# Tail of a one-layer hybrid decoder step: two of the last eight multiplications on POOL, their stores from ACT's queue, the last addition and square in halves

## The chip, the cores and the metric

The kernel runs on one core of a Trainium2 chip. The metric is the device time of one execution in microseconds, as the median of several runs. Five engines work side by side, each with its own instruction stream: PE (matrix multiplication), DVE (vector), ACT (scalar and activation functions), POOL (general SIMD) and SP (here it only issues DMAs). They meet only through semaphores. Matrix products are written to PSUM; everything else lives in SBUF, and outputs go to HBM by DMA.

## The reference, cut to what matters

One layer of a decoder: a normalised input goes through a projection, a gated convolution and a retention mixer, an output projection, and then a feed-forward block. The outputs are the final normalisation of the residual stream and the new states. The change lies wholly in the last two lines of this:

```python
x = x + concat([conv_out, ret_out]) @ w_out
xn = _rmsnorm(x, norm2_g)
x = x + (silu(xn @ w_gate) * (xn @ w_up)) @ w_down
...
# _rmsnorm(x, g): x * rsqrt(mean(x * x) + EPS) * g
y = _rmsnorm(x, final_norm_g)
```

## The kernel before, in words

The residual stream is held transposed: 1024 features as 8 row blocks (`m`, 0 to 7) of 128 partitions, and 1056 tokens as columns in two sets (`s`), each in two column groups (`g`). The last column group is `s` = 1, `g` = 1, with `n` = 256 columns. `x1[m][g]` holds the sum so far of a row block.

Nearly all of the time goes into matrix products in which each operand is split into a high and a low part, so that three products stand for one. The down projection is done in blocks of inner tiles; its last block, the loop over `s`, `g` and `m` at the end, takes 12 products per row block into a PSUM bank `ps` (line 1001). Then, for that row block, DVE adds the bank to `x` (line 1006), ACT squares `x` into `q` (`sq3`, line 1011; line 1008 for `m` = 0) and scales `x` by the gain of the final norm (line 1014), and DVE sums the squares into `ss3` (line 1013). The square of the last row block isn't added: it goes to the norm as a second operand.

`finish` normalises one column group. `rms_compact` (line 213) has PE multiply `ss3` and then `q`, 128 columns at a time, by a vector of ones: two products each, which bring the sum over partitions. DVE, ACT and DVE again make the reciprocal root from it, on 128x2 elements (lines 222, 224 and 198 to 202). PE spreads it over all partitions into the PSUM tile `pb`, called `n3b` in the trace (line 981). Then DVE multiplies each of the 8 row blocks by `pb` into `yt` (line 986), and after every two of them SP issues one store of 256 KB (line 987).

`finish` is a generator. Its steps for one column group are drawn between the products of the next group (`next(tail, None)`); those of the last group have no products left to hide behind. The framework that builds the program orders the instructions of each engine, finds out from the tiles what each must wait for, and puts in the semaphores. The `fin` pool keeps four `yt` buffers, and five small ones that `ss3` and `sq3` share. SP's stream ends with waits for all outstanding DMAs, and then all engines meet at a barrier (line 115).

Of the kernel before, what the change touches and what calls it, by code (L numbers as in the profile page):

```python
# [12 lines left out]
AF = mybir.ActivationFunctionType  # L13
ALU = mybir.AluOpType
AX = mybir.AxisListType

P = 128
# [14 lines left out]
KT = DM // P  # L32
# [6 lines left out]
SETS = 2  # L39
# [8 lines left out]
SO = [0, 272]  # L48
# [65 lines left out]
def _build(nc, t, offs, ncols):  # L114
    with tile.TileContext(nc) as tc:
        _body(nc, tc, t, offs, ncols)


def _body(nc, tc, t, offs, ncols):
    PSUM = bass.MemoryType.PSUM  # L120
    V, S, G, T, D = nc.vector, nc.scalar, nc.gpsimd, nc.tensor, nc.sync
    HW = SG // 2
    with contextlib.ExitStack() as ctx:
# [23 lines left out]
        gf = gains[:, 2 * KT:3 * KT]  # L147
# [15 lines left out]
        def split_w(ap, n=1024):  # L163
            return [split_u(load_w(ap[:, o:min(n, o + 512)], min(512, n - o)), min(512, n - o))
                    for o in range(0, n, 512)]
# [11 lines left out]
        def bank(name):  # L177
            return acc.tile([P, 2, 512], F32, tag="acc", name=name)
# [10 lines left out]
        def proj(w, xs, s, width, name, fill=None):  # L189
            ps = bank(name)  # L190
            for k in range(len(xs)):
                mm_k(ps, w, k, xs[k], s, width, k == 0, k == len(xs) - 1)
                if fill is not None and k % 2 == 1:
                    next(fill, None)
            return pg(ps, s, width)
# [8 lines left out]
        def rms_compact(sets, name):  # L204
            blocks = [(i, o, min(P, w - o)) for i, (_, w) in enumerate(sets) for o in range(0, w, P)]
            tot = len(blocks)
            ps = aux.tile([P, 512], F32, tag="aux", name=name + "p")
            a = cst.tile([P, 16], F32, tag="rms", name=name + "a", bufs=6)
            V.memset(a, 1.0)
            nq = len(sets[0][0])  # L210
            for q in range(nq):
                for i, (c, o, n) in enumerate(blocks):
                    T.matmul(ps[:n, q * tot + i:q * tot + i + 1], sets[c][0][q][:, o:o + n], ones[:, 0:1],
                             start=True, stop=True)
            for q in range(nq):
                i = 0
                while i < tot:
                    j, n = i, blocks[i][2]
                    while j < tot and blocks[j][2] == n:
                        j += 1  # L220
                    if q == 0:
                        V.tensor_scalar(a[:n, i:j], ps[:n, i:j], 1.0 / DM, EPS, ALU.mult, ALU.add)
                    else:
                        V.scalar_tensor_tensor(a[:n, i:j], ps[:n, q * tot + i:q * tot + j], 1.0 / DM, a[:n, i:j],
                                               ALU.mult, ALU.add)
                    i = j
            r = cst.tile([P, 16], F32, tag="rms", name=name + "r", bufs=6)
            tmp = cst.tile([P, 16], F32, tag="rms", name=name + "t", bufs=6)
            rsqrt(r[:, :tot], a[:, :tot], tmp[:, :tot])
            return r, blocks  # L230
# [17 lines left out]
        with contextlib.ExitStack() as mid_ctx:  # L248
# [74 lines left out]
            for k in range(KT):  # L323
                for s in range(SETS):
                    n = WALL[s]
# [25 lines left out]
            for s in range(SETS):  # L351
                n = WALL[s]
# [42 lines left out]
            for j in range(4):  # L395
                w = w_in(C_V + j)
                for s in range(SETS):
                    ps = proj(w, xn[s], s, WALL[s], "pv")
# [263 lines left out]
        def gg(name):  # L662
            return late.tile([P, SG], F32, tag="gg", name=name, bufs=9)
# [8 lines left out]
        for f in range(4):  # L672
            w = w_in(C_G + f)
            for s in range(SETS):
                n = WTOK[s]
                ps = proj(w, xn[s], s, n, "pg")
                x = gg("gt")
# [29 lines left out]
        for s in range(SETS):  # L707
            n = ntok[s]
            ss2 = late.tile([P, SG], F32, tag="rr", name="ss2", bufs=3)
            half = None  # L710
            for m in range(KT):
                x = gg("x1")
                D.dma_start(x[:, :2 * n], t["x"][m * P:(m + 1) * P, OFF[s]:OFF[s] + 2 * n])
                ps = proj(split_w(t["w_out"][m]), mix[s], s, 2 * n, "po")
# [28 lines left out]
                else:  # L743
                    q = gg("sq")
# [126 lines left out]
        x1 = [[None] * 2 for _ in range(KT)]  # L871
        for f in range(NFF):
# [34 lines left out]
            for g in range(2):  # L907
                x, y = gt[g][:, :HT], up[g][:, :HT]
# [19 lines left out]
        def tf(name):  # L928
            return fin.tile([P, HW], F32, tag="tt", name=name, bufs=5)
# [42 lines left out]
        yo = t["o_y"].rearrange("(m p) n -> p m n", p=P)  # L972

        def finish(s, g, ss3, q):
            n = ntok[s]
            oc = slice(OOFF[s] + g * n, OOFF[s] + (g + 1) * n)
            r, blocks = rms_compact([([ss3, q], n)], "n3")
            yield
            pb = aux.tile([P, 512], F32, tag="aux", name="n3b")
            for i, (_, o, w) in enumerate(blocks):  # L980
                T.matmul(pb[:, o:o + w], r[:w, i:i + 1].broadcast_to([w, P]), ident[:w, :w], start=True, stop=True)
            for m in range(0, KT, 2):
                yt = fin.tile([P, SG], F32, tag="yt", name="yt", bufs=4)
                y2 = yt[:, :2 * n].rearrange("p (g n) -> p g n", g=2)
                for i in range(2):
                    V.tensor_tensor(y2[:, i, :], x1[m + i][g][:, SO[s]:SO[s] + n], pb[:, :n], ALU.mult)
                D.dma_start(yo[:, m:m + 2, oc], y2)
                yield

        tail = iter(())  # L990
        for s in range(SETS):
            for g in range(2):
                n = ntok[s]
                ss3 = tf("ss3")
                for m in range(KT):
                    ps = bank("pd3")
                    hi, lo = wd[m]
                    for k in range(NPL):
                        sl = slice(k * P, (k + 1) * P)
                        for i, (wt, part) in enumerate(((hi, 0), (hi, 1), (lo, 0))):  # L1000
                            T.matmul(ps[:, 0, :n], wt[:, sl], hs[k][g][part][:, SO[s]:SO[s] + n],  # L1001
                                     start=(k == 0 and i == 0), stop=(k == NPL - 1 and i == 2))
                    if 1 <= m <= 6:
                        next(tail, None)
                    x = x1[m][g][:, SO[s]:SO[s] + n]
                    V.tensor_tensor(x, ps[:, 0, :n], x, ALU.add)
                    if m == 0:
                        S.activation(ss3[:, :n], x, AF.Square)
                    else:
                        q = tf("sq3")  # L1010
                        S.activation(q[:, :n], x, AF.Square)
                        if m < KT - 1:
                            V.tensor_tensor(ss3[:, :n], ss3[:, :n], q[:, :n], ALU.add)
                    S.activation(x, x, AF.Copy, scale=gf[:, m:m + 1])
                tail = finish(s, g, ss3, q)
# [64 lines left out]
```

## Time and profile before

| | |
|---|---|
| median of 3 runs | 1210.95 us |
| lowest and highest run | 1210.27 and 1212.86 us |
| time of the profiled execution | 1209.64 us |
| its span, first to last instruction | 1207.9 us |
| its mean granted TensorE clock | 0.996 |
| busy: PE, DVE, ACT, POOL | 98%, 70%, 40%, 10% |

The profiled execution takes 1.74 us more than its span, and lies 1.31 us below the median of the runs. Of the span, the last 10.5 us (from 1197.4 us) come after the last large product of PE. A busy share over the whole span says little of them: what ends last there must be read from the chain of waits, the timeline and the DMA windows of that stretch.

### The profile page before, as it was taken

How to read it: one execution, taken by the hardware profiler on the slowest of the kernel's cores; microseconds unless marked ns; L12 is line 12 of the kernel's file. 1: busy time of each engine (PE TensorE's matmuls, PEld its weight loads, DVE VectorE, ACT ScalarE, POOL GpSimd, SP SyncE). 2: the span in 40 equal slices, each digit the busy share in tenths (PEclk: the TensorE clock that was granted, in tenths of full speed). 3: DMA queues.
4: the chain of work that ended last, by engine and by line, in shares of the span. 5: the costliest groups of instructions: out<-in, count | busy, mean ns of one | idle time of the engine just before them, and what ended most of it. 6: DMA issues, size and time to landing. Idle time of an engine off the chain costs nothing.

```text
span 1207.9 us, 22799 instructions
## 1 busy us (share of the span) xinstructions
PE 1186.2 (98%) x8903; PEld 1133.1 (94%) x8903; DVE 844.8 (70%) x1591; ACT 487.2 (40%) x932; POOL 121.4 (10%) x251
## 2 busy tenths in 40 slices
PE   8999999999999999999999999999999899999997
PEld 7998978999989998899999999999999899999996
DVE  5455467676454577877787887787777588886656
ACT  8256531111233456544443444444344222222363
POOL 0100111000100012102211221122021100000000
PEclk9999999999999999999999999999999999999999
DMA  6321211001111355425434542454253998965213
GB/s 233 94 85 35 79 41 57 27 27 36 40 46 44 104 184 189 144 74 185 152 110 140 183 157 91 159 179 150 82 197 126 392 354 274 309 214 178 77 39 107
DMA packets 82060, 162.91 MB, mean 135 GB/s; under 512 B 10703, under 2 KB 23777, under 8 KB 81953
## 3 DMA queue, kind: packets, MB, share of 16 engines
q1 hardware_dynamic: 67568, 114.57, 29.1%
q0 software_dynamic: 14384, 46.88, 10.7%
q8 instruction: 70, 1.15, 0.4%
q14 instruction: 38, 0.30, 0.1%
HBM read 113.15 MB, written 48.26 MB: 134 GB/s over the span
## 4 chain that ended last, share of the span: by engine, by line
PE 84%; issue 7%; DMA 3%; DVE 3%; POOL 1%; ACT 1%; SPq 0%; DVEq 0%; POOLq 0%; ACTq 0%
PE by L768 17%; PE bz L768 8%; PE dy L768 8%; PE po L186 6%; PE bw L768 4%; PE pk L186 4%; PE pc L186 4%; PE pd L1001 4%; PE dz L768 4%; PE pg L186 4%; PE pq L186 4%; PE pv L186 4%; PE ph L186 4%; PE pb L186 3%; PE dw L768 2%
## 5 line engine op out<-in xcount | busy, mean ns | idle before, releaser
L158 ACT ACTIVATE whi<-wraw 128x512 fp32r<-128x512 f32 (+2 forms) x198 | 115.7, 585 | 285.5 <-issue 50.5
L160 DVE TENSOR_TENSOR wlo<-wraw,whi 128x512 fp32r<-128x512 f32 (+2 forms) x198 | 124.4, 629 | 48.4 <-ACT whi L158 48.3
L158 ACT ACTIVATE whi<-s 128x512 fp32r<-128x512 f32 (+2 forms) x152 | 83.7, 551 | 163.9 <-PE by L768 49.6
L768 PE MATMUL by<-t,whi 128*128 128x256 f32 (+1 forms) x704 | 130.7, 285 | 0.0
L768 PE MATMUL bz<-t,whi 128*128 128x256 f32 (+1 forms) x704 | 130.0, 283 | 0.0
L768 PE MATMUL by<-b,whi 128*128 128x256 f32 (+1 forms) x704 | 129.8, 284 | 0.1
L160 DVE TENSOR_TENSOR wlo<-s,whi 128x512 fp32r<-128x512 f32 (+2 forms) x152 | 89.4, 588 | 35.7 <-ACT whi L158 35.5
L768 PEld LDWEIGHTS by<-b,whi 128*128 128x128 f32 x704 | 109.3, 188 | 0.4 <-DVE up L896 0.3
L768 PEld LDWEIGHTS bz<-t,whi 128*128 128x128 f32 x704 | 109.0, 188 | 0.0
L768 PEld LDWEIGHTS by<-t,whi 128*128 128x128 f32 x704 | 108.9, 188 | 0.0
L768 PE MATMUL by<-b,wlo 128*128 128x256 f32 (+1 forms) x352 | 100.1, 284 | 0.0
L768 PE MATMUL bz<-t,wlo 128*128 128x256 f32 (+1 forms) x352 | 100.0, 284 | 0.0
L768 PE MATMUL by<-t,wlo 128*128 128x256 f32 (+1 forms) x352 | 99.8, 284 | 0.0
L768 PEld LDWEIGHTS by<-b,wlo 128*128 128x128 f32 x352 | 66.4, 189 | 0.0
L768 PEld LDWEIGHTS by<-t,wlo 128*128 128x128 f32 x352 | 66.3, 188 | 0.0
L768 PEld LDWEIGHTS bz<-t,wlo 128*128 128x128 f32 x352 | 66.3, 188 | 0.0
L768 PE MATMUL bw<-b,whi 128*128 128x272 f32 (+1 forms) x352 | 65.3, 284 | 0.0
L960 DVE TENSOR_TENSOR x<-x,dy 128x528 f32<-128x528 f32 x64 | 45.0, 703 | 25.6 <-PE dy L768 24.9
L794 POOL DMA_DIRECT2D hd<-hh x63 | 34.0, 540 | 270.8 <-ACT hh L792 265.1
L768 PE MATMUL dz<-ht,whi 128*128 128x256 f32 (+1 forms) x288 | 55.3, 289 | 3.6 <-ACT whi L158 3.6
L768 PE MATMUL dy<-hb,whi 128*128 128x256 f32 (+1 forms) x288 | 53.4, 284 | 2.4 <-ACT whi L158 2.0
L768 PE MATMUL dy<-ht,whi 128*128 128x256 f32 (+1 forms) x288 | 54.5, 286 | 0.2 <-issue 0.2
(303 smaller groups left out, 3087.1 us busy)
## 6 DMA issues: line engine op xcount, KB each, us to landing
ht<-hd SPq DMA_DIRECT2D x72, 264.0 KB, 5.3
hd<-hh POOLq DMA_DIRECT2D x63, 264.0 KB, 3.8
hd<-hl POOLq DMA_DIRECT2D x63, 264.0 KB, 3.9
hb<-hd SPq DMA_DIRECT2D x54, 264.0 KB, 5.4
wraw<-w_in SPq DMA_DIRECT2D x54, 256.0 KB, 2.6
wraw<-w_gate SPq DMA_DIRECT2D x44, 256.0 KB, 2.7
wraw<-w_up SPq DMA_DIRECT2D x44, 256.0 KB, 2.7
wraw<-w_out SPq DMA_DIRECT2D x32, 256.0 KB, 2.8
```

The costliest lines, as they stand in the source:

```text
L158: S.activation(hi[:, :n], raw[:, :n], AF.Copy)
L160: V.tensor_tensor(lo[:, :n], raw[:, :n], hi.bitcast(F32)[:, :n], ALU.subtract)
L186: T.matmul(ps[:, g, :n], wt[:, sl], xk[part][:, g * n:(g + 1) * n], start=(first and i == 0), stop=(last and i == 2))
L768: T.matmul(out, wt[:, sl], rhs(s, k, key, part), start=(first and k == 0 and i == 0), stop=(k == kt - 1 and i == 2), skip_group_check=not ...
L794: G.dma_start(dst[0], hi.bitcast(F32)[:, :HT])
L960: V.tensor_tensor(x, x, ps, ALU.subtract if i else ALU.add)
L1001: T.matmul(ps[:, 0, :n], wt[:, sl], hs[k][g][part][:, SO[s]:SO[s] + n], start=(k == 0 and i == 0), stop=(k == NPL - 1 and i == 2))
```

## The change

It is confined to the last column group (`s` = 1, `g` = 1), by the flag `last` and by a test on `m`.

```diff
+            last = s == SETS - 1 and g == 1
+            if last:
+                sb = tf("sb")
+                S.activation(sb[:, :n], pb[:, :n], AF.Copy)
+            for m in range(KT - 2, -1, -2) if last else range(0, KT, 2):
-            for m in range(0, KT, 2):
                 yt = fin.tile([P, SG], F32, tag="yt", name="yt", bufs=4)
                 y2 = yt[:, :2 * n].rearrange("p (g n) -> p g n", g=2)
                 for i in range(2):
-                    V.tensor_tensor(y2[:, i, :], x1[m + i][g][:, SO[s]:SO[s] + n], pb[:, :n], ALU.mult)
-                D.dma_start(yo[:, m:m + 2, oc], y2)
+                    x = x1[m + i][g][:, SO[s]:SO[s] + n]
+                    if last and m == KT - 2:
+                        G.tensor_tensor(y2[:, i, :], x, sb[:, :n], ALU.mult)
+                        S.dma_start(yo[:, m + i, oc], y2[:, i, :])
+                    else:
+                        V.tensor_tensor(y2[:, i, :], x, pb[:, :n], ALU.mult)
+                if not last or m < KT - 2:
+                    D.dma_start(yo[:, m:m + 2, oc], y2)
...
                     x = x1[m][g][:, SO[s]:SO[s] + n]
+                    if s == SETS - 1 and g == 1 and m == KT - 1:
+                        q = tf("sq3")
+                        for o in range(0, n, P):
+                            V.tensor_tensor(x[:, o:o + P], ps[:, 0, o:o + P], x[:, o:o + P], ALU.add)
+                            S.activation(q[:, o:o + P], x[:, o:o + P], AF.Square)
+                        S.activation(x, x, AF.Copy, scale=gf[:, m:m + 1])
+                        continue
```

ACT copies the spread reciprocal root from PSUM to `sb` in SBUF; POOL multiplies row blocks 6 and 7 by `sb`; ACT issues one store of 128 KB for each. DVE multiplies the other six, in the order 4, 5, 2, 3, 0, 1, and SP issues three stores of 256 KB. For row block 7, the addition and the square are done in two halves of 128 columns.

DVE's stream ended like this before, from the last step of the reciprocal root on (`x_10546` and `x_10550` are row blocks 0 and 1 of the last column group, `x_7_1_...` is row block 7, `n3r` the root; in brackets stand the semaphores that an instruction waits for):

```order
L202 SCALAR_TENSOR_TENSOR n3r<-n3t,n3r 128x2 [waits DVE_49]
L986 TENSOR_TENSOR yt<-x_10546,n3b 128x256 [waits DMAHW7_49,PE_49]
L986 TENSOR_TENSOR yt<-x_10550,n3b 128x256
L986 TENSOR_TENSOR yt<-x_2_1_11019,n3b 128x256 [waits DMAHW0_49]
L986 TENSOR_TENSOR yt<-x_3_1_11023,n3b 128x256
L986 TENSOR_TENSOR yt<-x_4_1_11179,n3b 128x256 [waits DMAHW1_49]
L986 TENSOR_TENSOR yt<-x_5_1_11183,n3b 128x256
L986 TENSOR_TENSOR yt<-x_6_1_11339,n3b 128x256 [waits DMAHW2_49]
L986 TENSOR_TENSOR yt<-x_7_1_11343,n3b 128x256
```

It ends like this now:

```order
L202 SCALAR_TENSOR_TENSOR n3r<-n3t,n3r 128x2 [waits DVE_49]
L995 TENSOR_TENSOR yt<-x_4_1_11179,n3b 128x256 [waits DMAHW0_49,Activation_49]
L995 TENSOR_TENSOR yt<-x_5_1_11183,n3b 128x256
L995 TENSOR_TENSOR yt<-x_2_1_11019,n3b 128x256 [waits DMAHW1_49]
L995 TENSOR_TENSOR yt<-x_3_1_11023,n3b 128x256
L995 TENSOR_TENSOR yt<-x_10546,n3b 128x256 [waits DMAHW2_49]
L995 TENSOR_TENSOR yt<-x_10550,n3b 128x256
```

The multiplications went from eight to six, and the first of them, which waited for PE, now waits for ACT: for the copy of the same PSUM bank into `sb`, which stands on ACT's stream after the root. ACT's stream ended with that root before; it now ends like this:

```order
L1020 ACTIVATE sq_14212<-x_7_1_11343 128x128 [waits DVE_49] x2
L1021 ACTIVATE x_7_1_11343<-x_7_1_11343,gains 128x256 [waits Activation_49]
L198 ACTIVATE n3t<-n3a 128x2 [waits DVE_49]
L985 ACTIVATE sb<-n3b 128x256 [waits PE_49]
L993 DMA o_y<-yt 128x256 [waits DMAHW3_49,Pool_49]
L993 DMA o_y<-yt 128x256 [waits DMAHW4_49,Pool_49]
```

Three instructions are added behind the root: the copy, and two stores that wait for POOL (and for the stores that last used the same semaphores).

## Rows read from the trace of the kernel before

**Rows 1.** The page: busy time, share of the span and instructions of each engine; and the shares of the span by engine in the chain that ended last.

```profile
PE 1186.2 (98%) x8903; PEld 1133.1 (94%) x8903; DVE 844.8 (70%) x1591; ACT 487.2 (40%) x932; POOL 121.4 (10%) x251
...
PE 84%; issue 7%; DMA 3%; DVE 3%; POOL 1%; ACT 1%; SPq 0%; DVEq 0%; POOLq 0%; ACTq 0%
```

**Rows 2.** The chain of waits in order of time, asked for from 1185 us on: start in us, us, engine, tile and line.

```profile
1191.14 6.26 PE pd L1001 x53
1197.40 0.02 issue
1197.43 0.43 DVE x L1006
1197.86 0.02 issue
1197.88 0.42 ACT sq L1011
1198.31 0.04 issue
1198.35 0.62 PE n3p L213 x4
1198.97 0.02 issue
1198.99 0.17 DVE n3a L222
...
1200.52 0.70 PE n3b L981 x4
1201.21 0.02 issue
1201.24 0.42 DVE yt L986
```

**Rows 3.** The timeline of the same stretch, in five answers: start, us, engine, line and operation, with the count of instructions merged into a row.

```profile
1196.79 0.89 ACT L1014 ACTIVATE x<-x,gains 128x256 f32<-128x256 f32 x2
...
1198.35 0.52 PEld L213 LDWEIGHTS n3p<-ones,sq 128*128 128x128 f32 x4 [0.38 <-ACT sq L1011]
...
1201.24 2.74 DVE L986 TENSOR_TENSOR yt<-x,n3b 128x256 f32<-128x256 f32 x8 [0.87 <-PE n3b L981]
...
1202.02 0.37 SPq L987 DMA_DIRECT2D o_y<-yt  x1
...
1204.00 0.37 SPq L987 DMA_DIRECT2D o_y<-yt  x1
```

**Rows 4.** Stretches of the end: length, then busy us (and instructions) of PE, weight loads, DVE, ACT and POOL, the granted TensorE clock, the mean busy share of the 16 DMA engines, and GB/s.

```profile
1202.00:1202.90 0.90, 0.00 (x0) 0.00 (x0) 0.90 (x3) 0.00 (x0) 0.00 (x0) 0.65 0.00 0
1202.90:1203.70 0.80, 0.00 (x0) 0.00 (x0) 0.80 (x4) 0.00 (x0) 0.00 (x0) 0.50 0.98 330
1203.70:1204.50 0.80, 0.00 (x0) 0.00 (x0) 0.28 (x1) 0.00 (x0) 0.00 (x0) 0.50 1.04 342
1204.50:1205.30 0.80, 0.00 (x0) 0.00 (x0) 0.00 (x0) 0.00 (x0) 0.00 (x0) 0.50 1.01 342
1205.30:1206.10 0.80, 0.00 (x0) 0.00 (x0) 0.00 (x0) 0.00 (x0) 0.00 (x0) 0.50 0.89 297
1206.10:1207.90 1.80, 0.00 (x0) 0.00 (x0) 0.00 (x0) 0.00 (x0) 0.00 (x0) 0.50 0.00 0
```

**Rows 5.** DMA issues: of the last 7 us, then two groups of the whole span, then one of the first 14 us (tile and source, queue, count, KB each, median us from issue to landing); the least, middle and longest landing of the last four stores.

```profile
o_y<-yt SPq DMA_DIRECT2D x4, 256.0 KB, 2.3
...
hd<-hh POOLq DMA_DIRECT2D x63, 264.0 KB, 3.8
...
o_sret<-sst POOLq DMA_DIRECT2D x8, 128.0 KB, 2.0
...
wraw<-w_in SPq DMA_DIRECT2D x5, 256.0 KB, 8.0
...
DMA to landing us min/median/max: 2.2/2.3/2.5
```

**Rows 6.** Groups by line and form over the whole span: busy us, mean ns of one, and the idle time before them. The last row is from the view of one line and gives the shortest, middle and longest of four instructions in ns.

```profile
L160 DVE TENSOR_TENSOR wlo<-s,whi 128x256 fp32r<-128x256 f32 x48 | 20.1, 419 | 0.8 <-ACT whi L158 0.8
...
L160 DVE TENSOR_TENSOR wlo<-s,whi 128x384 fp32r<-128x384 f32 x16 | 8.8, 552 | 0.1
...
L986 DVE TENSOR_TENSOR yt<-x,n3b 128x256 f32<-128x256 f32 x16 | 5.6, 415 | 1.1 <-PE n3b L981 1.1
...
L158 ACT ACTIVATE whi<-s 128x256 fp32r<-128x256 f32 x48 | 20.0, 417 | 58.9 <-DVE s L756 26.0 <-PE dy L768 25.1 <-PE dz L768 5.2
...
L158 ACT ACTIVATE whi<-s 128x384 fp32r<-128x384 f32 x16 | 8.4, 524 | 21.0 <-PE dy L768 14.5 <-PE dz L768 5.0 <-DVE s L756 1.4
...
L444 ACT ACTIVATE q<-pot 128x128 f32<-128x128 f32 x32 | 6.4, 277 | 6.3 <-PE pot L442 6.3
...
L387 ACT ACTIVATE v<-pvt 128x512 f32<-128x512 f32 x8 | 4.7, 588 | 2.1 <-PE pvt L386 2.1
...
L417 POOL MEMSET state<- 128x512 f32 x1 | 0.6, 552 | 0.0
...
masks.py:197 POOL MEMSET ident<- 128x128 f32 x1 | 0.2, 204 | 0.3 <-POOLq L1054 0.3
...
L626 POOL COPY sx<-stc x4: 200/660/1140, 46.0 to 312.0; 128x16 f32<-128x16 f32 x4
```

## The prediction, made before the changed kernel was run

> **What bounds the kernel now.** I read the page's shares first: PE is busy for 98% of the span and makes 84% of the chain that ended last [rows 1]. But the change touches nothing before the last column group, so I went on to the chain in order of time [rows 2]. There the reader is to see that PE's last long run of products ends at 1197.40 us and that everything behind it is a line of single steps: addition on DVE, square on ACT, sums on PE, root on DVE and ACT, spreading on PE until 1201.21, multiplications on DVE from 1201.24. The timeline gives the eight multiplications as one row of 2.74 us, and SP's first and last store of the group at 1202.02 and 1204.00 [rows 3]. The chain stops at DVE, and one would take the multiplications for the limit. The stretches of the end say otherwise [rows 4]: no byte moves before 1202.90, and from there until about 1206.05 the 16 DMA engines are busy without a gap (0.98, 1.04, 1.01 of their time) at some 340 GB/s. Four stores of 256 KB are 1.05 MB, and 1.05 MB in 3.15 us is 333 GB/s. The stores become ready one per 0.66 us (two multiplications; 1.98 us over three stores) and take 0.77 us each at 340 GB/s, so a queue forms. That is why landing takes from 2.2 to 2.5 us in this group [rows 5]. The last 1.85 us, to 1207.90, are receipts and the closing barrier. So the end is set by when the first bytes go on the wire, plus the bytes; when the last multiplication ends matters less.
>
> **The change part by part,** against the profiled execution (1209.64 us, of which 1207.90 are span).
>
> *Halves.* DVE takes 419 ns for 256 columns and 552 for 384, so 0.133 per 128 columns and 0.286 for 128 [rows 6]. Eight multiplications of 415 ns in 2.74 us start 0.332 apart [rows 3, 6], so 0.08 of each is covered by the next; the second half of the addition starts about 0.20 after the first. First half 1197.43 to 1197.72, second 1197.63 to 1197.92 (the whole one ended at 1197.86). ACT takes 417 and 524 ns for 256 and 384 columns, so 0.31 for 128 [rows 6], and two scalings of 0.50 in 0.89 us show that it too overlaps by about 0.12 [rows 3]. First square 1197.74 to 1198.05, second 1197.94 to 1198.25, against 1198.31 before [rows 2]. PE's four weight loads for the square take 0.52 us, 0.13 each [rows 3], the chain's 0.62 includes what follows the last load [rows 2]. With the first 128 columns there at 1198.09, their two loads are over at 1198.35; the other two and the rest take 0.62 − 0.26 = 0.36, to 1198.71 instead of 1198.97. Gain: 0.26 us. Bounds: the second half of the addition ends 0.06 later than the whole one did, and if nothing behind it overlapped, that would be the loss; with the second pair of loads starting at 1198.29, as the square alone would allow, 0.32. I take 0.26, since each overlap in it has a row. The scaling of row block 7 moves with the squares and still ends near 1198.8, ahead of the root at about 1199.1; it hides there as before.
>
> *Copy.* ACT reads 128 columns of PSUM in 277 ns and 512 in 588 [rows 6], so 0.38 for 256. The order of DVE's stream puts the first multiplication behind this copy, so all six wait for it, and the stores behind them: 0.38 plus a hand-off of 0.03. Nothing else is queued there. Cost 0.41 us. DVE begins at 1201.24 − 0.26 + 0.41 = 1201.39, the first SP store follows 0.78 later, as it does now (1202.02 − 1201.24), at 1202.17: 0.15 later than before. The last of three comes 2 × 0.66 later, at 1203.49 instead of 1204.00.
>
> *POOL.* No row has POOL multiply. A memset takes 204 ns for 128 columns and 552 for 512: 0.91 ns a column, so 0.32 us for 256 with one stream; that is the lower bound. POOL's slowest copy took 1.14 us, the upper [rows 6]. With two inputs I take the stream part twice: 0.09 + 2 × 0.23 = 0.55, near the memset rows, since the long copies have 16 columns only and can't be the price of a column. POOL starts with DVE at 1201.39, is done at 1201.94 and 1202.49, and ACT issues the two stores at 1201.97 and 1202.52. POOL has had nothing to do for a long while; the older waits in its stream are over. The Trainium skill, page "GPSIMD Engine Reference", section "3.1 Elementwise — side-by-side cycle accounting", counts some 2.6 cycles of 1.2 GHz per element for two inputs, an estimate of 0.555 us here; no run here shows it, and the sum by it would be the same.
>
> *ACT's queue.* The trace has no DMA issued from ACT. SP's issue takes 0.37 [rows 3]; landing is between 2.0 us (stores of 128 KB on POOL's queue) and 8.0 (loads when everything is asked for at once) [rows 5]. At the end nothing but these stores is on the wire, so I take SP's own behaviour, 0.88 us from issue to the first byte and 0.38 us on the wire.
>
> *Sum.* First bytes before: 1202.90, which is 0.88 behind SP's issue at 1202.02 [rows 3, 4]. Now: 1201.97 + 0.88 = 1202.85, from ACT's store; they last to 1203.23, and SP's first store is on the wire from 1203.05, so no gap follows. The bytes are the same, in packets of the same 1 KB rows. End −0.05 us, which is no change: 1209.6 in the profiled execution, 1210.9 on the median of the runs, which lies 1.31 above it. Two multiplications leave DVE (0.66 us), yet nothing of that reaches the end: it shortens a part that waits for the wire.
>
> Here the Trainium skill speaks against the change: "DMA: Bandwidth & Descriptors", section "Issuing engines are not separate DMA queues", says that DMAs from different engines run on the same 16 DMA engines and interleave, so that a second queue saves issue time alone. The share of 1.0 over three stretches [rows 4] agrees as far as one queue goes. By the rule the end stays, as in the sum; were it wrong, the first rival would hold.
>
> **The rivals.**
> 1. *The last store's latency sets the end, not the wire.* If two queues fill the DMA engines better than one, or the gaps between packets go, the end follows the last issue: 1203.49 for 1204.00, −0.51 us, 1210.4. For it: 0.66 us between stores is close to 0.77. Against: no gap in three stretches at 340 GB/s.
> 2. *The wait for the copy becomes the bound.* If the halves give nothing and POOL takes 1.14 us, the first store is SP's, at 1202.17 + 0.26 = 1202.43: +0.41, 1211.3. For it: the wait is in the order for certain, while the gain of the halves hangs on three engines overlapping. Against: each of these overlaps has a row.
> 3. *ACT's queue lands late (slower).* ACT's second store, issued at 1202.52, holds the end as soon as it takes longer than 3.98 us, since the last landing is now at 1204.00 + 2.5 = 1206.50. At the 8.0 us of the worst loads it is 4.0 us later: 1214.9. For it: a queue that is used for the first time. Against: the 8.0 us come from a crowd of loads, and POOL's stores with 3.8 at the median of a busy stage [rows 5] would still be in time.
> 4. *The change reaches further than its stretch.* If earlier work had been moved too, more than half a microsecond could go either way; but on every engine the instructions ahead of the last addition stand as they did.
>
> **How the numbers follow.** Forecast 0.54 (1210.9; its own mechanism allows 1210.6 to 1211.2), rival 1 0.25, rival 2 0.16, rival 3 0.04; 0.01 is left for the fourth. A measurement of this kernel tells about 0.2% from no change, 2.4 us. The whole stretch is 10.5 us long, and its rivals 1 and 2 move it by half a microsecond: both are "the same". Slower by more than 0.2% needs ACT's store to land after 6.4 us (rival 3, 0.03 of its 0.04), and 0.02 go to scatter; faster has only scatter, 0.03. So 0.03, 0.92, 0.05. The runs before spread from −0.7 to +1.9 around their median and the profiled one lies 1.3 below. From 1210.4 less 0.8 to 1211.3 plus 1.0: 1209.6 to 1212.3, with rival 3 left out.
>
> **What would show it.** In the profile after: PE's sums over the square end about 0.26 us sooner after the last product (1.31 instead of 1.57 us); ACT's copy of 0.38 us directly behind the spreading and DVE's first multiplication directly behind the copy; POOL's two multiplications near 0.55 us; first bytes about 5.4 us after the last product, as now (1202.90 − 1197.40 = 5.50), and DMA engines full for some 3.1 us. Wrong would be a wire with gaps and an end that follows the last issue (rival 1), first bytes more than 0.3 us later (rival 2), or a store of ACT among the last to land (rival 3).

## The result, and the profile after

The changed kernel takes 1214.57 us, the median of 7 runs (1213.54 to 1219.47), against 1210.90 us for the kernel before (7 runs, 1209.95 to 1212.86). The ratio is 1.0034, with a 95% interval from 1.0018 to 1.0050: slower by 3.7 us, where no change was forecast, and outside the range of the forecast (1209.6 to 1212.3). The profiled execution took 1213.96 us, its span is 1212.2 us.

The chain of waits in order of time answers to [rows 2] (start, us, engine, tile and line):

```profile
1191.64 6.26 PE pd L1011 x53
1197.91 0.02 issue
1197.93 0.30 DVE x L1019
1198.23 0.02 issue
1198.26 0.32 ACT sq L1020
1198.57 0.04 issue
1198.62 0.62 PE n3p L213 x4
...
1200.79 0.69 PE n3b L981 x4
1201.48 0.02 issue
1201.50 0.39 ACT sb L985
1201.89 0.02 issue
1201.92 0.42 DVE yt L995
```

PE's last large product ends at 1197.90, 0.5 us later than before; that is scatter of the work ahead. I therefore call the time from this point to the end of the span the *tail*: 1207.90 − 1197.40 = 10.50 us before, 1212.2 − 1197.9 = 14.3 us after. The whole loss, 3.8 us, lies in it. Yet the chain reads as forecast: the sums over the square end 1.34 us after the product (1.57 before), the copy takes 0.38 (0.39 in the chain), DVE begins 4.02 us after the product instead of 3.84.

The timeline of POOL, ACT's queue and SP's queue:

```profile
1201.97 1.42 POOL L992 TENSOR_TENSOR yt<-x,sb 128x256 f32<-128x256 f32 x2 [244.68 <-ACT sb L985]
...
1202.74 1.04 ACTq L993 DMA_DIRECT2D o_y<-yt  x2
...
1202.70 1.70 SPq L997 DMA_DIRECT2D o_y<-yt  x3
```

And the stretches of the end, which answer to [rows 4] (length, busy us and instructions of PE, weight loads, DVE, ACT, POOL, granted TensorE clock, share of the 16 DMA engines, GB/s):

```profile
1203.50:1203.60 0.10, 0.00 (x0) 0.00 (x0) 0.10 (x2) 0.00 (x0) 0.00 (x0) 0.50 0.16 51
1203.60:1204.40 0.80, 0.00 (x0) 0.00 (x0) 0.39 (x2) 0.00 (x0) 0.00 (x0) 0.50 0.99 323
1204.40:1205.20 0.80, 0.00 (x0) 0.00 (x0) 0.00 (x0) 0.00 (x0) 0.00 (x0) 0.50 1.01 344
1205.20:1206.00 0.80, 0.00 (x0) 0.00 (x0) 0.00 (x0) 0.00 (x0) 0.00 (x0) 0.50 1.02 338
1206.00:1206.80 0.80, 0.00 (x0) 0.00 (x0) 0.00 (x0) 0.00 (x0) 0.00 (x0) 0.50 0.91 300
1206.80:1207.20 0.40, 0.00 (x0) 0.00 (x0) 0.00 (x0) 0.00 (x0) 0.00 (x0) 0.50 0.00 0
1207.20:1211.40 4.20, 0.00 (x0) 0.00 (x0) 0.00 (x0) 0.00 (x0) 0.00 (x0) 0.50 0.00 0
```

The wire is full from 1203.6 to about 1206.8, about as long as before and without a gap. The bytes are out 8.9 us after the product, against 8.65 before. By 1207.2 the last store has landed, and then come 4.2 us in which no engine computes and no byte moves. What SP waits for at the end, by the view of waits (total us, times, longest us):

```profile
SPq L115 <- PEq L115: 4.8, 2, 4.3
SPq L115 <- DMA o_y<-yt: 2.3, 3, 1.3
```

Line 115 is the closing barrier. PE's name stands in the row because a barrier is many engines' doing; PE had nothing left to do since 1201.5. The view of line 115 tells whose instruction lasts (instruction, count, shortest/middle/longest in ns, first and last start); of after:

```profile
L115 POOLq DRAIN  x3: 40/102/9481, 1201.9 to 1211.9; - x3
L115 SPq DRAIN  x3: 7/7/7, 1207.2 to 1211.7; - x3
...
L115 ACTq DRAIN  x2: 8/80/151, 1203.8 to 1211.7; - x2
```

and the same rows of before, ahead of them POOL's last DMA issue from the timeline:

```profile
956.36 0.54 POOL L795 DMA_DIRECT2D hp<-hl  x1
...
L115 POOLq DRAIN  x3: 93/188/10657, 956.3 to 1207.5; - x3
L115 SPq DRAIN  x3: 7/7/7, 1206.6 to 1206.9; - x3
```

POOL's stream ends with a DRAIN, behind which it opens the barrier. After, it starts with the multiplications at 1201.9 and lasts 9.48 us, to 1211.4: 8.0 us beyond the second multiplication (1201.97 + 1.42 = 1203.39). SP has been there since 1207.2, all others earlier. Before, the DRAIN was no shorter, 10.66 us, some 10.0 of them beyond POOL's last instruction; but that was a DMA issue at 956 us, and the DRAIN was over 240 us ahead of the end. Nothing in the added code takes 4 us; it moved POOL's last instruction to where its DRAIN shows.

### The profile page after: what moved, and what is told of

Read it like the earlier page. It is cut to its first block, busy times and chain, and to the rows that moved or that the text cites. A ratio compares the mean times of both kernels' runs of the same rounds, so it can differ in the third digit from the quotient of the medians.

```text
span 1212.2 us, 22808 instructions
## 1 busy us (share of the span) xinstructions
PE 1186.8 (98%) x8903; PEld 1133.4 (94%) x8903; DVE 844.2 (70%) x1590; ACT 487.6 (40%) x934; POOL 123.4 (10%) x253
## 3 DMA queue, kind: packets, MB, share of 16 engines
q0 software_dynamic: 14384, 46.88, 10.8%
## 4 chain that ended last, share of the span: by engine, by line
PE 94%; DVE 2%; ACT 2%; DMA 1%; issue 0%; SPq 0%; DVEq 0%; ACTq 0%
PE by L768 21%; PE bz L768 11%; PE dy L768 8%; PE po L186 8%; PE bw L768 5%; PE dz L768 4%; PE pc L186 4%; PE pd L1011 4%; PE pg L186 4%; PE pq L186 4%; PE pv L186 4%; PE ph L186 3%; PE pb L186 3%; PE pk L186 3%; PE dw L768 2%; PE po L569 1%
```

## The experiments

Two theories. *D:* POOL's closing DRAIN ends some 8 us after POOL's last instruction, whatever that is, and holds the barrier. *Q:* ACT's queue, used for the first time, holds the closing. Both stand in the expectations, with the tail as their measure.

**One: DVE in POOL's place, everything else kept.**

```diff
-                        G.tensor_tensor(y2[:, i, :], x, sb[:, :n], ALU.mult)
+                        V.tensor_tensor(y2[:, i, :], x, sb[:, :n], ALU.mult)
```

> The tail is the span from the end of PE's last large product to the last instruction: 10.50 us before (1207.90 - 1197.40), 14.29 after (1212.2 - 1197.91). This kernel is the changed one with row blocks 6 and 7 multiplied by DVE from sb; ACT's copy, ACT's two stores and the halves stay. Theory D (POOL's closing DRAIN ends some 8 us after POOL's last computing instruction and holds the closing barrier): POOL's DRAIN ends near 967 us, the tail is 10.3 to 11.0 us, the time that of before within 0.1%. Theory Q (ACT's queue, used for the first time, holds the closing): the tail stays near 14.3 us, the time 0.3% above before.

Measured: ratio 1.0009 (0.9994 to 1.0023), tail 1208.8 − 1197.8 = 11.0 us. The loss is gone with ACT's queue in use. Its two stores land within 1.8 us, and POOL's DRAIN stands behind its last DMA issue again:

```profile
L115 POOLq DRAIN  x3: 102/188/10883, 957.0 to 1208.4; - x3
```

Of the 11.0 us, 0.5 belong to PE, whose spreading took 1.21 us instead of 0.69 (last section).

**Two: POOL kept, its stores issued by SP.**

```diff
-                        S.dma_start(yo[:, m + i, oc], y2[:, i, :])
+                        D.dma_start(yo[:, m + i, oc], y2[:, i, :])
```

> The changed kernel with POOL's two row blocks stored from SP's queue, so that ACT issues no DMA. Theory D: POOL's DRAIN still ends some 8 us after its second multiplication, the tail stays at 14 to 15 us and the time 0.3% above before. Theory Q: the tail goes back to 10.3 to 11.0 us and the time to that of before.

Measured: 1.0033 (1.0022 to 1.0044), tail 1213.3 − 1198.5 = 14.8 us (again with 0.5 of PE's). The loss stays without any store from ACT, and POOL's DRAIN again lasts 8.0 us beyond the multiplications:

```profile
1203.07 1.42 POOL L992 TENSOR_TENSOR yt<-x,sb 128x256 f32<-128x256 f32 x2 [244.41 <-ACT sb L985]
...
L115 POOLq DRAIN  x3: 40/93/9476, 1203.0 to 1213.0; - x3
```

Theory Q falls.

**Three: the kernel before with one tiny instruction of POOL.**

```diff
+                if s == SETS - 1 and g == 1 and m == 0:
+                    G.tensor_copy(tf("z")[:, :1], y2[:, 0, :1])
                 D.dma_start(yo[:, m:m + 2, oc], y2)
```

> The kernel before with a single addition: POOL copies one column of the first finished product of the last group into a scratch tile, which nobody reads. Theory D: the copy runs some 5 us behind the last product, the DRAIN ends some 8 us later, so the tail is 12.5 to 14.5 us instead of 10.50, +2 to +4 us (0.2 to 0.3%), for a copy of some 0.2 us. Theory Q: no change, 10.5 us. If only long or two-input instructions of POOL drag a DRAIN behind them: no change either.

Measured: 1.0031 (1.0012 to 1.0050), tail 1210.6 − 1196.4 = 14.2 us. The two rows from the timeline and from the view of line 115:

```profile
1201.64 0.19 POOL L988 COPY z<-yt 128x1 f32<-128x1 f32 x1 [245.14 <-DVE yt L986]
...
L115 POOLq DRAIN  x3: 40/93/8214, 1201.6 to 1210.3; - x3
```

A copy of 0.19 us, off every chain, costs as much as the whole change. 8.21 − 0.19 = 8.0 us again: the price is the same behind a copy of one column as behind two multiplications.

**Four: the same POOL work one column group sooner.**

```diff
-            last = s == SETS - 1 and g == 1
+            last = s == SETS - 1 and g == 0
```

> The changed kernel with the flag set for the column group before the last: POOL's multiplications, ACT's copy and ACT's stores run there, some 10 us earlier, and DVE multiplies all eight row blocks of the last group; the halves stay in the last group. Theory D: the DRAIN still takes 8 us or more from POOL's last instruction, but is over near 1201 to 1203 us, ahead of the last bytes, so the tail is 10.0 to 10.7 us and the time that of before within 0.1%. Theory Q: ACT's queue has been used, so the tail stays near 14.3 us.

Measured: 0.9992 (0.9981 to 1.0004). POOL's rows:

```profile
1192.94 1.62 POOL L992 TENSOR_TENSOR yt<-x,sb 128x256 f32<-128x256 f32 x2 [235.16 <-ACT sb L985]
...
L115 POOLq DRAIN  x3: 40/93/9679, 1192.9 to 1208.4; - x3
L115 SPq DRAIN  x3: 7/7/7, 1207.8 to 1208.1; - x3
```

The DRAIN ends at 1192.9 + 9.7 = 1202.6, 8.0 us after the second multiplication, and ahead of the last bytes. It costs nothing there. Tail 9.9 us, a little under what was expected. The sums are no reason for that: they had to wait for DVE and ended 1.5 us after the product. The closing is: from SP's first DRAIN to the end of the span it takes 0.8 us here (1207.8 to 1208.6), and took 1.3 before (1206.6 to 1207.9).

**Five: the last store from POOL's own queue.** The kernel before, with one line changed:

```diff
-                D.dma_start(yo[:, m:m + 2, oc], y2)
+                (G if s == SETS - 1 and g == 1 and m == KT - 2 else D).dma_start(yo[:, m:m + 2, oc], y2)
```

> The kernel before with the last of the four last stores issued by POOL instead of SP. Theory D, with the DRAIN of before as its measure (10.66 us from about the start of POOL's last DMA issue): the DRAIN begins near 7 us behind the last product and ends some 10 to 11 us later, so the tail is 17 to 19 us, 7 us or more above before, 0.5 to 0.7%. If the 8 us belong to computing instructions alone and the long DRAIN of before only waited for its DMAs: the DRAIN ends with the store's landing some 2.5 us after the issue, and the tail stays at 10.5 to 11.5 us.

Measured: 1.0061 (1.0042 to 1.0080), tail 1216.7 − 1199.7 = 17.0 us.

```profile
1207.12 0.72 POOL L987 DMA_DIRECT2D o_y<-yt  x1 [247.85 <-DVE yt L986]
...
L115 POOLq DRAIN  x3: 40/93/8822, 1207.1 to 1216.4; - x3
```

8.82 − 0.72 = 8.1 us behind a DMA issue as well. It was expected at 10 to 11 us by the row of before; where the 2 us more of that DRAIN come from, no run shows. The store itself landed after 2.6 us, well ahead of the DRAIN's end.

**Six: POOL computes late, but has issued no DMA.** The changed kernel, with each of POOL's 204 DMAs issued by SP:

```diff
-            G.dma_start(dst[0], hi.bitcast(F32)[:, :HT])
+            D.dma_start(dst[0], hi.bitcast(F32)[:, :HT])
...
```

> The changed kernel with every DMA of POOL issued by SP instead, so that POOL only computes; the two multiplications at the end stay on POOL. What its time does in the middle is not asked; its closing is. If the 8.0 us between POOL's last instruction and the end of its DRAIN belong to any late instruction of POOL: a DRAIN of 9.4 to 9.7 us again, closing near 8.6 us after the second multiplication. If they are housekeeping for the DMAs that POOL issued earlier: a DRAIN of less than 2 us, and a closing that follows the last landing as in the kernel before (1.4 us behind it).

Measured: the two rows of POOL's end, and SP's waits:

```profile
1207.72 1.42 POOL L992 TENSOR_TENSOR yt<-x,sb 128x256 f32<-128x256 f32 x2 [854.58 <-ACT sb L985]
...
L115 POOLq DRAIN  x3: 34/77/1482, 1207.7 to 1213.7; - x3
...
SPq L115 <- DMA o_y<-yt: 2.8, 1, 2.8
SPq L115 <- PEq L115: 0.6, 2, 0.4
```

The same two multiplications, and the DRAIN is over with them, 1.48 us after it began. The closing follows the stores, tail 1214.0 − 1203.1 = 10.9 us. So the 8 us are paid for the DMAs that POOL issues in the course of the kernel (in the changed kernel the last of them 245 us ahead of the multiplications), and not for a late instruction as such. (The time, 1.0023 with an interval from 1.0007 to 1.0038, is that of a kernel whose SP has 204 more DMAs in its queue, and says nothing of the end.)

**Seven to nine: how many DMAs.** The same, with one, 142 and 62 of the 204 left on POOL (the "some 170" of the first expectation is a miscount): the load of the table; the spills of the feed-forward block; all others. Each was executed once, for its trace. Against the sixth kernel, the first of them is

```diff
-            D.dma_start(tab, t["tab"])
+            G.dma_start(tab, t["tab"])
```

and the second does the same to the two DMAs of `to_hd`; the third is the changed kernel with these two on SP.

> The changed kernel with all DMAs of POOL issued by SP except one, the load of the table near 100 us; the two multiplications at the end stay on POOL. If the 8 us in the closing DRAIN come as soon as POOL has issued any DMA: a DRAIN of 9.4 to 9.7 us. If they grow with the number of DMAs (some 170 in the changed kernel): a DRAIN near the 1.48 us of the kernel without any. With no DMA on POOL it was 1.48 us, no longer than the multiplications behind which it stands.

> The changed kernel in which POOL keeps the 142 spill DMAs of the feed-forward block and SP issues the other 62. Read is the time from the end of POOL's second multiplication to the end of its closing DRAIN: 8.0 us with 204 DMAs on POOL, about 0.1 us with one and with none. If it grows with their number, 39 ns each (8.0 / 204): 5.5 to 5.7 us. If it is one price for all kernels with more than a few: 8.0 us.

> The reverse: POOL keeps the 62 other DMAs, all before the feed-forward block, and SP issues the 142 spills. If the time grows with the number of DMAs: 2.3 to 2.6 us, so that the DRAIN ends ahead of the last store's landing, and the closing follows the stores. If one price for all: 8.0 us. If only the spills late in the kernel count: about 0.1 us.

The rows, in this order, each with its multiplications ahead:

```profile
1205.24 1.42 POOL L992 TENSOR_TENSOR yt<-x,sb 128x256 f32<-128x256 f32 x2 [853.70 <-ACT sb L985]
...
L115 POOLq DRAIN  x3: 40/89/1588, 1205.2 to 1211.3; - x3
```

```profile
1207.52 1.42 POOL L992 TENSOR_TENSOR yt<-x,sb 128x256 f32<-128x256 f32 x2 [245.45 <-ACT sb L985]
...
L115 POOLq DRAIN  x3: 40/102/4449, 1207.5 to 1213.4; - x3
```

```profile
1205.78 1.42 POOL L992 TENSOR_TENSOR yt<-x,sb 128x256 f32<-128x256 f32 x2 [687.70 <-ACT sb L985]
...
L115 POOLq DRAIN  x3: 40/102/6621, 1205.7 to 1212.9; - x3
```

Less the 1.42 us of the multiplications (and, for the last, 0.04 by which the DRAIN begins ahead of them): 0.17 us for one DMA, where none left 0.06, 3.0 for 142, and 5.15 for 62. One price for all is refuted, and so is a price per DMA: 21 ns in the one set, 83 in the other. But the two sets add up to 8.2, where all 204 gave 8.0. This fits a price to which DMAs add unequal shares; that every DMA has one is not shown. What sets the shares stays open: POOL's queue moved 11360 packets in the set that costs less and 3024 in the other, so the packets alone don't.

**Ten: the halves alone,** on the kernel before.

```diff
+                    if s == SETS - 1 and g == 1 and m == KT - 1:
+                        q = tf("sq3")
+                        for o in range(0, n, P):
+                            V.tensor_tensor(x[:, o:o + P], ps[:, 0, o:o + P], x[:, o:o + P], ALU.add)
+                            S.activation(q[:, o:o + P], x[:, o:o + P], AF.Square)
+                        S.activation(x, x, AF.Copy, scale=gf[:, m:m + 1])
+                        continue
```

> The kernel before with the halves alone (no copy, no POOL, no store from ACT). By the step on the halves: PE's sums over the square end 1.31 to 1.35 us after the last large product instead of 1.57, everything behind them 0.2 to 0.3 us sooner, the tail 10.2 to 10.3 us where PE's clock is at its full level for the spreading, and 0.5 us more where it is at half (spreading 0.7 or 1.2 us). POOL's DRAIN near 967 us. Time the same as before within 0.1%. If the halves bring nothing: 1.57 us and a tail of 10.5 us (or 11.0).

The rows of the product and of the sums:

```profile
1193.15 6.26 PE pd L1001 x53
...
1200.12 0.62 PE n3p L213 x4
```

Measured: sums at 1.33 us after the product, as expected; tail 1210.2 − 1199.4 = 10.8, with the spreading at 1.21 us. Ratio 0.9992 (0.9978 to 1.0007). The quarter microsecond is there and can't be told in the time.

**Eleven and twelve: what would help the end.** First bytes sooner, by single stores, on the kernel before with the halves; first of the first pair alone, then of all eight row blocks (there without `and m == 0`):

```diff
+                single = s == SETS - 1 and g == 1 and m == 0
...
-                D.dma_start(yo[:, m:m + 2, oc], y2)
+                    if single:
+                        (S if i else D).dma_start(yo[:, m + i, oc], y2[:, i, :])
+                if not single:
+                    D.dma_start(yo[:, m:m + 2, oc], y2)
```

> The kernel before with the halves and with the first pair of the last group stored as two single row blocks of 128 KB, the first from SP and the second from ACT; all eight multiplications on DVE, no copy. If the end is the first bytes plus the bytes: the first store is issued 0.33 us sooner after the first multiplication begins (0.45 instead of 0.78), the DMA engines fill from there without a gap, and the tail is 9.8 to 10.1 us (10.4 to 10.6 with the spreading at half clock). If the last store's latency sets the end: tail as with the halves alone, 10.2 to 10.3 us (or 10.8). The time against before: 0.9990 to 1.0005, hardly to be told from 1.

Measured: tail 1208.5 − 1198.47 = 10.0 us, ratio 1.0004 (0.9992 to 1.0016). The stretch in which the first bytes move:

```profile
1203.00:1203.50 0.50, 0.00 (x0) 0.00 (x0) 0.50 (x3) 0.00 (x0) 0.00 (x0) 1.00 0.24 84
```

That is some 4.9 us after the product, 0.6 sooner than before. The last store was issued 0.25 us sooner (6.35 us after the product instead of 6.6), and the tail is shorter by 0.5: in these two profiles it follows the first bytes rather than the last issue.

> The kernel before with the halves, and with all eight row blocks of the last group stored singly (128 KB each), by SP and ACT in turn; DVE does all eight multiplications. If the end is the first bytes plus the bytes, and no gap is left on the wire: in the kernel with only the first pair single the wire was nearly empty for about 0.25 us between the second and the third store, so the tail goes from 10.03 to 9.7 to 9.9 us (10.2 to 10.4 if PE's clock has fallen before the spreading). If the single stores cost the wire time of their own: 10.0 us or more. Against the kernel before the time is 0.9985 to 1.0005; 0.7 us of 1211 are 0.06%, so the tail decides, not the ratio.

Measured: tail 1208.2 − 1198.07 = 10.1 us, ratio 1.0001 (0.9990 to 1.0012). Expected were 9.7 to 9.9. No gap is left on the wire, which was empty some 8.0 us after the product instead of 8.2, and the last store landed sooner too, at 8.5 us instead of 8.7. SP lost it again: it takes its closing waits one after another, and when the last store had landed (at 1206.55 us of this trace) it still had these ahead of it:

```profile
L115 SPq EVENT_SEMAPHORE  x6: 28/28/28, 1206.6 to 1206.9; - x6
```

It was through with them 0.4 us behind the landing; with the first pair alone single, 0.1 us behind it. Both tails are shorter than that of the kernel before by some 0.4 us, which is 0.03% and not measurable in the time; no version here beats it beyond its interval.

## Why the prediction was wrong

**The step that failed** is in the first part: "The last 1.85 us, to 1207.90, are receipts and the closing barrier." I took them for a fixed piece that hangs on the last landing alone. The closing hangs on every engine, and POOL's way to it was 8.0 us long from its last instruction. The part on POOL has the same mistake in other words: "POOL has had nothing to do for a long while; the older waits in its stream are over." The waits were; what its DMAs leave to the closing DRAIN was not. The size follows from the runs: POOL's last instruction ends 5.5 us after the product and its DRAIN 8.0 later, at 13.5; SP is ready at 9.3. That is 4.2 us. SP was ready 0.1 us later than before, and what follows took 0.8 us instead of 1.3, so 3.8 remain. Why the last part is shorter where POOL computes late (the fourth run has the same 0.8), no run shows.

The sign of it could have been read: the row of the 10.66 us DRAIN is in the trace of before, in the view of the barrier's line. That the price comes again behind any later instruction of POOL, only the runs could tell. I looked at what SP waits for at the end, not at what each engine still has to do after its last computing instruction, since on the page such instructions don't count as busy. The Trainium skill, page "VectorE: DVE Perf Modes", section "The DRAIN you can't avoid", gives some 12 ns, constant on all five engines, for the DRAINs that the runtime puts ahead of and behind a program. The one here belongs to line 115 of the program itself and took 9481 ns, so that figure doesn't cover it; no trace here shows those of the runtime.

**What held.** The halves: 0.26 us forecast, 0.23 after and 0.24 in the tenth run (1.34 and 1.33 us for 1.57). The copy: 0.38 forecast, 0.38 measured, and DVE behind it as the order showed; its first multiplication comes 0.18 us later than before, forecast 0.15. The wire: full for 3.2 us with two queues, 3.1 with one. So the first rival, that two queues fill it better or the last issue sets the end, is out: SP's last store was issued 6.1 us after the product instead of 6.6, and the bytes were out later all the same; the eleventh run moved the first bytes and the end went with them. Bytes out 0.25 us later than before, where −0.05 was forecast.

**What was off in size.** POOL's multiplication was taken at 0.55 us; two of them take 1.42, 0.71 each. The estimate by the Trainium skill, page "GPSIMD Engine Reference", section "3.1 Elementwise — side-by-side cycle accounting", was 0.555; the trace doesn't agree, and the measurement decides. The first store of ACT was issued 0.27 us later against the product than worked out for this, and makes up most of the 0.3 us on the wire.

**The rivals.** The second, with the copy's wait as the bound, was in the right direction, and on the wire all delays together came to 0.25 us of the 3.8; by its own sign, first bytes more than 0.3 us later, it did not hold (5.7 us after the product for 5.5). The third had the right size, 4.0 us, for a wrong reason: ACT's stores landed within 3.1 us, and the second run has the loss without them. None of the four had POOL's closing in it, and the chance of slower, 0.05, was put on the wrong mechanism.

## What to carry to other kernels

Before giving late work to an idle engine, look at what stands behind its last instruction: in the view of the barrier's line, each engine's DRAIN, its length and its start. A POOL that issues DMAs has a long one (here 8.0 us for 204 DMAs); where POOL's last instruction ended far enough ahead of the last landing, in the fourth run, it cost nothing, and later even a copy of one column cost microseconds. And where the stores of a tail fill the wire, ask first when the first byte goes out: here that moved the end, and the last issue did not.

## What the runs showed of the hardware that I had not expected

- POOL's closing DRAIN ended 8.0 to 8.1 us after its last instruction in five kernels with 204 or 205 DMAs on POOL, behind multiplications, a copy of 0.19 us or a DMA issue, and within 0.2 us of it with one DMA or none. In the five kernels in which POOL's last instruction is a DMA issue at 956 to 959 us it ended 10.0 to 10.2 us behind that; the 2 us between are unexplained.
- In the tail the granted TensorE clock falls from 1.00 to 0.50 (of 2.4 GHz, so to 1.2 GHz), in some profiled executions only after the spreading and in others ahead of it. The spreading takes 0.69 or 1.21 us accordingly, and half a microsecond of scatter comes from that alone. In the first experiment, PE's last work before the fall was the sums, which end near 1199.1:

```profile
1199.00:1199.50 0.50, 0.12 (x2) 0.03 (x1) 0.31 (x2) 0.20 (x1) 0.00 (x0) 1.00 0.00 0
1199.50:1200.00 0.50, 0.00 (x0) 0.00 (x0) 0.20 (x3) 0.20 (x1) 0.00 (x0) 0.75 0.00 0
1200.00:1200.50 0.50, 0.00 (x0) 0.00 (x0) 0.43 (x3) 0.00 (x0) 0.00 (x0) 0.50 0.00 0
1200.50:1201.00 0.50, 0.32 (x1) 0.35 (x2) 0.03 (x1) 0.00 (x0) 0.00 (x0) 0.50 0.00 0
```

- A queue used for the first time was no slower: ACT's stores of 128 KB took 0.34 to 0.39 us to issue, and landed in 1.8 us where the wire was free (first experiment), as SP's did (second).
